# A bias table by distance: eight rows stored to DRAM, then spread to 128 rows by a DRAM-to-DRAM copy, issued in the first half of the projections

## The chip, the cores and the metric

The kernel runs on 1 core of one Trainium2 chip. The metric is the device time in microseconds (us) of one launch, as the median of 3 runs. One launch computes one inference step of a two-layer streaming encoder; weights, caches and inputs lie in DRAM at its start, and all outputs lie there at its end.

## The reference, cut to what matters

Layer 0 projects 2048 prompt frames and 64 sample frames, and mixes them in two branches. Branch A is latent attention (queries and keys are made by up-projections of small latents). Branch B is attention in a band of 9 chunks of 64 frames, with a learned bias per head that depends only on the clipped distance of query and key:

```
def _rel_bias(table, rel):                       # table: 8 heads x 257 distances
    idx = jnp.clip(rel, -B_MAX_REL, B_MAX_REL) + B_MAX_REL     # B_MAX_REL = 128
    return jnp.expand_dims(jnp.moveaxis(table[:, idx], 0, -3), -3)
...
    s = einsum(q, k) * scale + bias              # 64 queries x 576 keys, per head and chunk
```

Layer 1 is windowed attention without such a bias. What concerns the change is how the kernel gets the 8 x 257 table into a form from which it can load, for one head, a tile of 128 query rows whose row q is the row of biases shifted by q.

## The kernel before, in words

The program has five stages. Phase 1 projects the frames for layer 0; phase 2 is branch A, from about 845 us of the trace on; phase 3 is branch B with the output projection; two more do layer 1. All arithmetic on TensorE is done with each operand split in a high and a low part of float32r, and three products of them (`mm3`). All DMAs are issued by SyncE (`dma = nc.sync.dma_start`), one instruction after the other; an instruction that waits holds all behind it.

Phase 1 works in two halves of the frames, three chunks of 256 to 384 frames each. For a chunk, `norm_chunk` loads up to three tiles of 128 frames (tiles `R`, pool `raw`, 5 buffers, which the weight loads of `load_w` use too), takes sums of squares on ScalarE (line 251), makes the reciprocal roots on VectorE (`rstd_of`, lines 182 to 193), scales the rows (line 259), transposes them on TensorE (line 263) and splits them into the tile `X` (lines 207 and 210). Then come, for each half: the gate columns and the columns of the latent of the keys (`ckv`, 288 columns, tile `kcs` of rotary factors), the latent up-projections (`ukv`), the query latent (`qlat`) and its up-projection (`uq`), which loads a tile named `qcs` of rotary factors from a pool of one buffer, the queries and keys of branch B, its values (`vb`), and the last gate columns. Each result goes from PSUM (pool `pm`, 4 buffers) through a buffer of the pool `ev` (7 buffers) into a scratch tensor in DRAM: `sQA`, `sKA`, `sKR`, `sQR`, `sQB`, `sKB`, `sVB`, `sG`. A buffer of `ev` is free when its store has landed. The last keys of branch B are written out as a state too, by way of a transpose of an `ev` tile (line 489).

After the two halves, phase 1 makes the table `sE` (8 heads x 128 rows x 768 floats, 3 MB): the 257 biases of a head, reversed, go into partition h of a tile `e8` (named `qcs`, so it takes the same one buffer), VectorE repeats the first of them 511 times to the left (line 582), and one DMA writes each partition's row 128 times into `sE` (line 583). Phase 3 is its only reader; it loads `bias` tiles with a step that shifts row q by q.

The instructions are written in program order, but within phase 1 and across its border to phase 2 their order on each engine is set by the framework's planner, which simulates durations and issues what is ready first; phase 2's loads (lines 200, 622, 624, 637) are so put among phase 1's last stores. In phase 2 itself TensorE, VectorE and ScalarE follow the order as written.

Of the kernel before, what the change touches and what calls it, by code (L numbers as in the profile page):

```python
# [7 lines left out]
F32 = mybir.dt.float32  # L8
# [62 lines left out]
def tok_tiles(c0, n):  # L71
    r = []
    o = 0
    while o < n:
        w = min(128, n - o)
        r.append((c0 + o, o, w))
        o += w
    return r
# [29 lines left out]
def kernel(ctx, tc, a, o, upto=5):  # L108

    nc = tc.nc  # L110
    S = K()
    dma = nc.sync.dma_start
# [7 lines left out]
    def scratch(name, shape):  # L120
        return dr.tile(shape, F32, name=name)
# [9 lines left out]
    sQB = scratch("sQB", [2, 8, 64, SEQ])  # L131
    sKB = scratch("sKB", [2, 8, 64, SEQ])
    sVB = scratch("sVB", [8, SEQ, 128])
    sE = scratch("sE", [8, 128, 768])
    sM = scratch("sM", [512, T])
    sMB = scratch("sMB", [512, T])
# [31 lines left out]
    def load_row(t, src):  # L168

        dma(t, bass.AP(tensor=src.tensor, offset=src.offset, ap=[[0, 128], [1, t.shape[-1]]]))  # L170
        return t
# [40 lines left out]
    def load_w(pw, raw, src, kt, w, slot):  # L212

        W = pw.tile([128, slot], F32R, name="W")
        Wv = W[:, :2 * kt * w].rearrange("p (a k c) -> p a k c", a=2, k=kt)
        sv = src.rearrange("(k p) c -> p k c", p=128)
        step = max(1, 1024 // w)
        for k0 in range(0, kt, step):
            k1 = min(kt, k0 + step)
            R = raw.tile([128, 1024], F32, name="R")  # L220
            Rv = R[:, :(k1 - k0) * w].rearrange("p (k c) -> p k c", c=w)
            dma(Rv, sv[:, k0:k1])
            nc.scalar.activation(Wv[:, 0, k0:k1], Rv, AF.Copy)  # L223
            nc.gpsimd.tensor_tensor(Wv[:, 1, k0:k1], Rv, Wv[:, 0, k0:k1], op=ALU.subtract)  # L224
        return Wv

    def mm3(ps, lhs, rhs, kt):

        n = 3 * kt
        j = 0  # L230
        for k in range(kt):
            for x, y in TERMS:
                nc.tensor.matmul(ps, lhs(x, k), rhs(y, k), start=(j == 0), stop=(j == n - 1))  # L233
                j += 1
# [37 lines left out]
    def phase1():  # L272
        with ExitStack() as st:
            pool = pools(st, "right")
            lat, xin, rows, tb = pool("lat", 1), pool("xin", 2), pool("rows1", 1), pool("tb", 1)
# [8 lines left out]
            def first_loads():  # L284
                load_row(g_pre, a["ab_pre_norm"])
                dma(ident, a["ident"])

            def later_loads():
                load_row(g_kv, a["ab_kv_norm"])
                dma(kcs, a["krope"])  # L290
                load_row(g_q, a["ab_q_norm"])
# [13 lines left out]

            def ukv(W, cT, c_off, col0, n, vrow=None):


                for o0, w in even_split(n, 512, 64):
                    for j in range(4):  # L310
                        p = pm.tile([128, 512], F32, name="pm")
                        mm3(p[:, :w], lambda x, k: W[:, x, k, j * 128:(j + 1) * 128],
                            lambda y, k: cT[:, y, k, c_off + o0:c_off + o0 + w], 2)
                        hi = ev.tile([128, 512], F32R, name="ev")
                        lo = ev.tile([128, 512], F32R, name="ev")
                        copy(hi[:, :w], p[:, :w])
                        lo_of(lo[:, :w], p[:, :w], hi[:, :w])
                        for x, t in ((0, hi), (1, lo)):
                            dma(head_pair(sKA, x, j, col0 + o0, w), f(t[:, :w]))
                        yield  # L320

            def ukv_v(W, cT, c_off, t0, r, vrow):
                p = pm.tile([128, 512], F32, name="pm")
                mm3(p[:r], lambda x, k: cT[:, x, k, c_off:c_off + r], lambda y, k: W[:, y, k, 512:1024], 2)
                if vrow is None:
                    for h0 in (0, 4):
                        v_out(p[:, h0 * 64:h0 * 64 + 256], r, t0, None, h0, 4, sVA)
                else:
                    e = ev.tile([128, 512], F32, name="ev")
                    copy(e[:r], p[:r])  # L330
                    dma(sVS[vrow:vrow + r], e[:r])
# [170 lines left out]
            def build_x(c):  # L502
                Xs[c] = x_chunk(*c)

            def fs_piece(chunks, col, specs, after=None):
                for _ in fs_steps(chunks, col, specs, after):
                    pass

            def weave(main, other, lead, rate):

                acc = 0.0
                for i, _ in enumerate(main):
                    if i >= lead - 1:
                        acc += rate
                    while acc >= 1:
                        next(other, None)
                        acc -= 1
                for _ in other:
                    pass

            def latents(W, cT, hf):
                hb = HBASE[hf]
                yield from ukv(W, cT, 0, hb, HLEN[hf])
                for t0, off, r in tok_tiles(hb, HLEN[hf]):
                    ukv_v(W, cT, off, t0, r, 0 if t0 >= SEQ else None)
                    yield
                if hf == 1:
                    yield from cached(W)

            def fs_steps(chunks, col, specs, after=None):  # L530
                W = load_w(pw, raw, w_in[:, col:col + 128 * len(specs)], KT, 128 * len(specs), SLOT)
                for i, c in enumerate(chunks):
                    if c not in Xs:
                        build_x(c)
                    for jj, (kind, j) in enumerate(specs):
                        fs(W, Xs[c], jj, c[0], c[1], kind, j)
                        yield
                    if after:
                        build_x(after[i])

            build_x(CHUNKS[0])
            for hf in range(2):
                chunks, hb = HALVES[hf], HBASE[hf]
                main = fs_steps(chunks, 672, kinds[0:3])
                cT = lat.tile([128, 2, 2, 1088], F32R, name="lat")
                for i, c in enumerate(chunks):
                    for _ in range(3):
                        next(main)
                    if i == 0:
                        if hf == 0:  # L550
                            later_loads()
                        W = load_w(pw, raw, w_in[:, 384:672], KT, 288, SLOT)
                    if i + 1 < len(chunks) and chunks[i + 1] not in Xs:
                        build_x(chunks[i + 1])
                    ckv(W, Xs[c], c[0], c[1], cT, hb)
                main = fs_steps(chunks, 1056, kinds[3:6])
                next(main)
                W = load_w(pw, raw, a["w_ukv"], 2, 1024, SLOT)
                weave(main, latents(W, cT, hf), LD1[hf], RT1[hf])
                W = load_w(pw, raw, w_in[:, 0:384], KT, 384, SLOT)  # L560
                qT = lat.tile([128, 2, 3, 1088], F32R, name="lat")
                for c in chunks:
                    qlat(W, Xs[c], c[0], c[1], qT, hb)
                main = fs_steps(chunks, 1440, kinds[6:9])
                next(main)
                W = load_w(pw, raw, a["w_uq"], 3, 768, SLOT)
                weave(main, uq(W, qT, hb, chunks), LD2, RT2)
                fs_piece(chunks, 1824, kinds[9:12])
                for h0 in (0, 4):
                    W = load_w(pw, raw, w_in[:, 2208 + h0 * 64:2208 + h0 * 64 + 256], KT, 256, SLOT)  # L570
                    for c in chunks:
                        vb(W, Xs[c], c[0], c[1], h0)
                Ws = [load_w(pw, raw, w_in[:, col:col + 256], KT, 256, SLOT) for col in (2720, 2976)]
                for i, c in enumerate(chunks):
                    for j in range(4, 8):
                        fs(Ws[(j - 4) // 2], Xs[c], j % 2, c[0], c[1], "g", j)
                    if hf == 0:
                        build_x(HALVES[1][i])

            e8 = tb.tile([128, 768], F32, name="qcs")  # L580
            dma(e8[:8, 511:768], a["rel"])
            nc.vector.tensor_copy(e8[:8, 0:511], e8[:8, 511:512].to_broadcast([8, 511]))
            dma(sE, e8[:8, None].to_broadcast([8, 128, 768]))
            dma(o[11][448:512], vbs)
            for src, dst in ((a["cache_b_k"], o[10]), (a["cache_b_v"], o[11])):
                dma(dst[0:448], src[64:512])
# [1049 lines left out]
    def phase5():  # L1636

        with ExitStack() as st:
# [261 lines left out]
            with manual(M5, ORDERED | {mybir.EngineType.SP}):  # L1900
# [10 lines left out]
                J.tails.drain()  # L1911

    phase1()
    P3 = phase3()
    S.start3 = lambda: next(P3) if upto >= 3 else None
# [100 lines left out]
```

## Time and profile before

| | us |
|---|---|
| median of 3 runs | 2776.84 (2775.26 to 2778.05) |
| the profiled execution, its own time | 2781.05 |
| its span in the trace | 2779.1 |
| TensorE busy (matmul) | 2581.4, 93% of the span |
| VectorE, ScalarE, GpSimd busy | 1474.4, 1391.1, 774.1 |

[...] A busy share over 1 in the DMA column means that packets of several transfers overlap on an engine. GB/s counts what DRAM gave and what it took, so that a copy inside DRAM counts twice.

### The profile page before, as it was taken

The page shows a single profiled execution, that of the slowest core. Times are in us where ns is not written, and L with a number is a line of the kernel's source. Part 1 is how long each engine was busy: PE and PEld are TensorE (multiplying, and loading weights), DVE is VectorE, ACT ScalarE, POOL GpSimd, SP SyncE. Part 2 cuts the span into 40 slices and gives each one's busy share as a digit, 9 for nine tenths or more (in the row PEclk, how much of TensorE's full clock was granted, in tenths as well). Part 3 has the DMA queues.
Part 4 walks back from the last instruction along what each step waited for, and adds up shares of the span by engine and source line. Part 5 has one row for each costly group of instructions (what it writes and reads, how often), then busy time and mean ns, then how long its engine had stood idle before and what let it go on. Part 6 is the DMA issues. An engine that isn't in the chain of part 4 may idle for free. (4 is left out here: it accounts for less than half of the span.)

```text
span 2779.1 us, 46736 instructions
## 1 busy us (share of the span) xinstructions
PE 2581.4 (93%) x16296; PEld 2352.2 (85%) x16296; DVE 1474.4 (53%) x4048; ACT 1391.1 (50%) x3547; POOL 774.1 (28%) x1311
## 2 busy tenths in 40 slices
PE   7999999999399999999888989988999999999997
PEld 7999999898398888888757878878999998788886
DVE  5542155351006777777646777735213102788884
ACT  4332232422126777777656666652233222777784
POOL 1123222213012333321202313364213220244444
PEclk9999999999699999999979999999999998999999
DMA  6546444727626666662287776655535428455552
GB/s 200 169 146 206 127 140 142 240 87 201 137 89 172 181 190 176 189 179 77 70 252 191 191 195 184 194 188 188 170 101 169 130 68 244 103 132 136 144 132 70
DMA packets 382259, 437.91 MB, mean 158 GB/s; under 512 B 49920, under 2 KB 308872, under 8 KB 378792
## 3 DMA queue, kind: packets, MB, share of 16 engines
q1 hardware_dynamic: 382024, 434.92, 54.1%
q8 instruction: 130, 2.13, 0.3%
q14 instruction: 105, 0.86, 0.1%
HBM read 279.65 MB, written 157.07 MB: 157 GB/s over the span
## 5 line engine op out<-in xcount | busy, mean ns | idle before, releaser
L233 PE MATMUL pm<-X,W 128*128 128x384 f32 (+2 forms) x4536 | 752.8, 325 | 1.7 <-DVE ev L210 0.9
L233 PEld LDWEIGHTS pm<-X,W 128*128 128x128 f32 x4536 | 731.9, 189 | 4.4 <-DVE ev L210 1.1
L207 ACT ACTIVATE PT<-t 128x512 fp32r<-128x512 f32 (+3 forms) x704 | 343.8, 505 | 255.1 <-PE t L1192 96.2
L210 DVE SCALAR_TENSOR_TENSOR PT<-t,PT 128x512 fp32r<-128x512 f32 (+3 forms) x688 | 374.8, 569 | 97.9 <-ACT PT L207 95.2
L224 POOL TENSOR_TENSOR W<-R,W 128x768 fp32r<-128x768 f32 (+3 forms) x114 | 233.3, 2073 | 591.9 <-ACT W L223 539.2
L953 PE MATMUL proj<-Wo,MM 128*128 128x512 f32 (+1 forms) x1368 | 378.9, 406 | 4.2 <-POOL MM L1739 1.5
L210 DVE SCALAR_TENSOR_TENSOR ev<-pm,ev 128x384 fp32r<-128x384 f32 (+3 forms) x197 | 98.7, 503 | 518.6 <-ACT ev L1543 180.3
L233 PE MATMUL pm<-W,X 128*128 128x256 f32 (+5 forms) x2040 | 283.9, 299 | 0.7 <-DVE ev L210 0.7
L953 PEld LDWEIGHTS proj<-Wo,MM 128*128 128x128 f32 (+1 forms) x1368 | 235.4, 185 | 48.6 <-ACT z L207 4.6
L233 PEld LDWEIGHTS pm<-W,X 128*128 128x128 f32 (+1 forms) x2040 | 274.5, 188 | 2.1 <-DVE ev L210 0.9
L691 ACT ACTIVATE P<-s,m 128x512 f32<-128x512 f32 (+9 forms) x344 | 209.5, 616 | 32.6 <-DVE m L680 30.1
L672 PE MATMUL s<-KA,Q 128*128 128x512 f32 (+7 forms) x640 | 201.1, 397 | 9.1 <-ACT P L691 8.9
L715 PE MATMUL t<-ident,P 128*128 128x128 f32 x1088 | 176.3, 276 | 3.4 <-ACT P L691 1.0
L678 DVE TENSOR_REDUCE m<-s 128x1 f32<-128x480 f32 (+7 forms) x216 | 132.5, 613 | 81.0 <-PE s L672 80.6
L715 PEld LDWEIGHTS t<-ident,P 128*128 128x128 f32 x1088 | 134.7, 141 | 41.5 <-ACT P L691 15.0
L743 PE MATMUL acc<-PT,V 128*128 128x256 f32 x1152 | 156.1, 285 | 6.5 <-DVE OT L752 6.5
L743 PEld LDWEIGHTS acc<-PT,V 128*128 128x128 f32 x1152 | 140.4, 188 | 12.0 <-PE t L715 6.0
L207 ACT ACTIVATE ev<-pm 128x256 fp32r<-128x256 f32 (+7 forms) x117 | 51.3, 440 | 158.8 <-PE pm L233 72.1
L1686 ACT ACTIVATE P<-s,m 128x256 f32<-128x256 f32 (+2 forms) x264 | 119.7, 467 | 6.9 <-DVE m L1678 5.6
L223 ACT ACTIVATE W<-R 128x768 fp32r<-128x768 f32 (+3 forms) x114 | 97.9, 908 | 47.1 <-DMA R<-in_ab_w_in_dram 18.9
L1205 PE MATMUL acc<-PT,V 128*128 128x256 f32 x672 | 114.1, 302 | 4.9 <-DVE OT L1215 3.8
L672 PE MATMUL s<-KR,Q 128*128 128x384 f32 (+6 forms) x320 | 116.3, 363 | 2.1 <-DMA Q<-sQR 2.1
(249 smaller groups left out, 4068.3 us busy)
## 6 DMA issues: line engine op xcount, KB each, us to landing
Q<-sQA SPq DMA_DIRECT2D x128, 128.0 KB, 3.0
sWO<-W SPq DMA_DIRECT2D x32, 512.0 KB, 3.7
Q<-sQB SPq DMA_DIRECT2D x128, 128.0 KB, 3.4
Wo<-sWO SPq DMA_DIRECT2D x16, 1024.0 KB, 7.5
Q<-sQC SPq DMA_DIRECT2D x32, 512.0 KB, 7.7
R<-in_ab_w_in_dram SPq DMA_DIRECT2D x40, 384.0 KB, 3.8
K<-sKB SPq DMA_DIRECT2D x56, 256.0 KB, 5.4
V<-sVB SPq DMA_DIRECT2D x24, 512.0 KB, 6.4
```

What stands on the lines that cost most here:

```text
L207: nc.scalar.activation(out, in_, AF.Copy)
L210: nc.vector.scalar_tensor_tensor(out, x, scale, hi, op0=ALU.mult, op1=ALU.subtract)
L224: nc.gpsimd.tensor_tensor(Wv[:, 1, k0:k1], Rv, Wv[:, 0, k0:k1], op=ALU.subtract)
L233: nc.tensor.matmul(ps, lhs(x, k), rhs(y, k), start=(j == 0), stop=(j == n - 1))
L672: nc.tensor.matmul(s[:r, :n], self.Q[:, x, self.qo:self.qo + r], rhs, start=(x == 0), stop=(x == 2))
L678: nc.vector.tensor_reduce(m[:r, j:j + 1], s[:r, :n], axis=AX.X, op=ALU.max)
L691: nc.scalar.activation(self.P[:r, o0:o0 + n], self.s.pop(j)[:r, :n], AF.Exp, bias=self.m[:r, 6:7], accum_out=acc)
L715: nc.tensor.transpose(t[:, b], self.P[:, (b0 + b) * 128:(b0 + b + 1) * 128], ident)
L743: nc.tensor.matmul(acc[:, (i // 2) % 2], H.V[:, b0 + b], PT[:, x, b], start=(b0 + b == 0 and x == 0), stop=(b0 + b == i and x == 1))
L953: nc.tensor.matmul(p, M[:, x, k, :r], W[k][:, y, cs], start=(k == k0 and t == 0), stop=(k == k1 - 1 and t == 2))
L1205: nc.tensor.matmul(acc, self.H.V[:, self.base - self.H.b0 + b], self.PT[:, x, off + b], start=(b == 0 and x == 0), stop=(b == nblk - 1 and ...
L1686: nc.scalar.activation(self.P[:, c, :w], self.s[:, c, :w], AF.Exp, bias=m[:, 1, c:c + 1], accum_out=m[:, 0, c:c + 1])
```

## The change

A scratch tensor `sE1` of 8 x 768 floats is added. The table is made by a function `biases_by_distance`, called in the first half, after the weights of the latent up-projections are loaded: the tile `e8` is filled as before, its eight rows are stored once into `sE1` (24 KB), and `sE` is filled by one copy from DRAM to DRAM, whose outermost dimension is the 128 rows (source step 0), then the 8 heads, then 768 floats in a run. The five lines after the second half go.

```diff
+    sE1 = scratch("sE1", [8, 768])
     sE = scratch("sE", [8, 128, 768])
...
+            def biases_by_distance():
+
+                e8 = tb.tile([128, 768], F32, name="qcs")
+                dma(e8[:8, 511:768], a["rel"])
+                nc.vector.tensor_copy(e8[:8, 0:511], e8[:8, 511:512].to_broadcast([8, 511]))
+                dma(sE1, e8[:8])
+                dma(sE.rearrange("h q e -> q h e"),
+                    bass.AP(tensor=sE1.tensor, offset=sE1.offset, ap=[[0, 128], [768, 8], [1, 768]]))
...
                 W = load_w(pw, raw, a["w_ukv"], 2, 1024, SLOT)
+                if hf == 0:
+                    biases_by_distance()
                 weave(main, latents(W, cT, hf), LD1[hf], RT1[hf])
...
-            e8 = tb.tile([128, 768], F32, name="qcs")
-            dma(e8[:8, 511:768], a["rel"])
-            nc.vector.tensor_copy(e8[:8, 0:511], e8[:8, 511:512].to_broadcast([8, 511]))
-            dma(sE, e8[:8, None].to_broadcast([8, 128, 768]))
             dma(o[11][448:512], vbs)
```

Nothing else of the source differs, but the planner's order does. On SyncE, at the start of the program, before:

```order
L432 DMA qcs<-in_qrope_dram 128x2x384
L586 DMA out_dram<-in_cache_b_k_dram 16x14336
L586 DMA out_dram<-in_cache_b_v_dram 16x14336
L1524 DMA out_dram<-in_cache_c_k_dram 16x512
L1525 DMA out_dram<-in_cache_c_v_dram 16x512
L222 DMA R<-in_ab_w_in_dram 128x2x384 x2
L222 DMA R<-in_ab_w_in_dram 128x3x288 x2
L222 DMA R<-in_ab_w_in_dram 128x2x288
L249 DMA R<-in_x_prompt_dram 128x1024 x4
```

and in the changed kernel (`sE_67` is how the name `sE1` is printed there):

```order
L292 DMA qcs<-in_rel_dram 8x257
L593 DMA out_dram<-in_cache_b_k_dram 16x14336
L593 DMA out_dram<-in_cache_b_v_dram 16x14336
L1531 DMA out_dram<-in_cache_c_k_dram 16x512
L1532 DMA out_dram<-in_cache_c_v_dram 16x512
L223 DMA R<-in_ab_w_in_dram 128x2x384 x2
L294 DMA sE_67<-qcs 8x768
L223 DMA R<-in_ab_w_in_dram 128x3x288 x2
L223 DMA R<-in_ab_w_in_dram 128x2x288
L295 DMA sE<-sE_67 128x8x768
L442 DMA qcs<-in_qrope_dram 128x2x384
L250 DMA R<-in_x_prompt_dram 128x1024 x4
```

The planner has moved the three DMAs of the table ahead of the loads of the second chunk's frames (the four loads of `R` from the prompt: three tiles of chunk 2, one of chunk 3), well before the place at which the source names them.

On ScalarE, at the place where chunk 2's sums of squares (`sq`, with the number of the sums' tile, 344 before and 345 now) stand among the gate outputs (`ev`) and the latents' sums (`c`), before:

```order
L251 ACTIVATE sq,ss_344<-R 128x1024 x2
L475 ACT_TABLE_LOAD
L475 ACTIVATE ev<-pm 128x384
L251 ACTIVATE sq,ss_344<-R 128x1024
L475 ACTIVATE ev<-pm 128x384
L251 ACTIVATE sq,ss_691<-R 128x1024
L475 ACTIVATE ev<-pm 128x384
```

and now:

```order
L485 ACT_TABLE_LOAD
L485 ACTIVATE ev<-pm 128x384 x3
L252 ACTIVATE sq,ss_345<-R 128x1024
L363 ACTIVATE c,ss<-pm 128x256
L252 ACTIVATE sq,ss_345<-R 128x1024 x2
L363 ACTIVATE c,ss<-pm 128x256
L252 ACTIVATE sq,ss_692<-R 128x1024 x2
```

The sums of squares of chunk 2 now stand behind the three gate outputs and, for the last two, behind the first latent's sum. On VectorE the chain of chunk 2's roots (128x3), alone before, is now woven row by row with two chains of the latents (128x1).

On SyncE at the end of phase 1, among the stores of branch B's keys (`sKB`), before:

```order
L419 DMA sKB<-ev 128x384 x3
L583 DMA sE<-qcs 1024x1x768
L622 DMA KA<-sKA 64x2112
L419 DMA sKB<-ev 128x384
L624 DMA KR<-sKR 128x2112
L419 DMA sKB<-ev 128x384 x5
```

and now:

```order
L429 DMA sKB<-ev 128x384 x3
L644 DMA Q<-sQR 64x512 x2
L429 DMA sKB<-ev 128x384
L629 DMA KA<-sKA 64x1024
L429 DMA sKB<-ev 128x384
L629 DMA KA<-sKA 64x1024
L631 DMA KR<-sKR 128x1024
L629 DMA KA<-sKA 64x2112 x2
L429 DMA sKB<-ev 128x384
L631 DMA KR<-sKR 128x2112
```

The table's store is gone, and phase 2's loads of keys, part of which stood ahead of this place before, now stand here, closer together.

## Rows read from the trace of the kernel before

**Rows 1.** The page: span, and busy time of the engines.

```profile
span 2779.1 us, 46736 instructions
PE 2581.4 (93%) x16296; PEld 2352.2 (85%) x16296; DVE 1474.4 (53%) x4048; ACT 1391.1 (50%) x3547; POOL 774.1 (28%) x1311
```

**Rows 2.** Busy time by stretch around the end of phase 1; columns: stretch, its length, busy time and count on PE, PEld, DVE, ACT, POOL, then TensorE's granted clock, the DMA engines' share, GB/s.

```profile
673.00:677.00 4.00, 1.51 (x10) 1.19 (x9) 0.56 (x1) 1.17 (x3) 0.00 (x0) 1.00 0.79 231
...
690.00:741.00 51.00, 0.49 (x4) 0.23 (x2) 0.56 (x1) 0.12 (x1) 0.00 (x0) 0.56 0.53 92
741.00:747.00 6.00, 5.68 (x27) 5.68 (x28) 0.85 (x2) 3.82 (x10) 4.26 (x2) 0.51 0.66 212
```

**Rows 3.** Who waited for whom between 640 and 800 us, longest first; the last row is from the same view of SyncE's queue.

```profile
DVE ev L210 <- DMA sKB<-ev: 71.1, 3, 60.2
...
PE po L489 <- ACT ev L207: 53.3, 2, 50.8
SPq L419 <- DMA sE<-qcs: 12.9, 1, 12.9
```

**Rows 4.** SyncE's queue in order of time, 655 to 745 us: start, length of the issue, engine, line, operation, target<-source, count.

```profile
669.10 0.81 SPq L583 DMA_DIRECT2D sE<-qcs  x1
672.19 7.28 SPq L622 DMA_DIRECT2D KA<-sKA  x1
679.57 18.16 SPq L419 DMA_DIRECT2D sKB<-ev  x1
697.78 4.77 SPq L624 DMA_DIRECT2D KR<-sKR  x1
702.65 32.84 SPq L419 DMA_DIRECT2D sKB<-ev  x5
```

**Rows 5.** Time from issue to landing, in us, from the views of one tile: first the loads of phase 2's keys `KA` between 640 and 800 us (the longest is the one issued at 672.19), then the stores of branch B's keys `sKB` between 640 and 680 us.

```profile
DMA to landing us min/median/max: 7.3/7.7/65.3
...
DMA to landing us min/median/max: 2.9/8.1/9.2
```

**Rows 6.** TensorE in order of time, 670 to 760 us.

```profile
680.87 9.63 PE L233 MATMUL pm<-X,W 128*128 128x320 f32 x64
741.32 0.47 PE L489 MATMUL po<-ident,ev 128*128 128x128 f32 x1 [50.83 <-ACT ev L207]
741.45 8.02 PE L233 MATMUL pm<-W,X 128*128 128x256 f32 x45
...
755.86 3.11 PE L233 MATMUL pm<-W,X 128*128 128x256 f32 x24
```

**Rows 7.** Busy time by stretch, columns as in rows 2: three stretches at the program's start, then the burst of phase 2's loads, the table's store alone, the clock's fall and its rise.

```profile
4.00:6.00 2.00, 0.00 (x0) 0.00 (x0) 0.50 (x4) 1.15 (x2) 0.00 (x0) 1.00 0.90 212
13.00:14.00 1.00, 0.00 (x0) 0.00 (x0) 1.00 (x4) 0.05 (x1) 1.00 (x2) 1.00 1.91 787
...
30.00:32.00 2.00, 2.00 (x13) 2.00 (x13) 0.00 (x0) 0.68 (x2) 2.00 (x2) 1.00 0.82 244
...
667.00:670.00 3.00, 3.00 (x19) 3.00 (x18) 0.56 (x1) 0.49 (x1) 0.00 (x0) 1.00 1.16 368
...
691.00:694.00 3.00, 0.00 (x0) 0.00 (x0) 0.00 (x0) 0.00 (x0) 0.00 (x0) 1.00 0.46 49
694.00:697.00 3.00, 0.00 (x0) 0.00 (x0) 0.00 (x0) 0.00 (x0) 0.00 (x0) 0.78 0.46 49
...
745.00:748.00 3.00, 3.00 (x20) 3.00 (x20) 0.00 (x0) 0.48 (x2) 2.48 (x2) 0.69 0.59 171
```

**Rows 8.** The DMA view of 0 to 40 us: target<-source, count, KB each, median us from issue to landing. The first is a copy inside DRAM, the second a load of one row of 4 KB into 128 partitions.

```profile
out_dram<-in_cache_b_k_dram SPq DMA_DIRECT2D x1, 896.0 KB, 9.6
...
g_pre<-in_ab_pre_norm_dram SPq DMA_DIRECT2D x1, 512.0 KB, 5.4
```

**Rows 9.** The first 52 us in order of time: SyncE's queue, then ScalarE, VectorE and TensorE (four answers of the same view, columns as in rows 4).

```profile
13.02 10.23 SPq L222 DMA_DIRECT2D R<-in_ab_w_in_dram  x5
26.15 6.17 SPq L249 DMA_DIRECT2D R<-in_x_prompt_dram  x4
...
35.28 1.05 ACT L251 ACTIVATE sq<-R 128x1024 bf16<-128x1024 f32 x1
...
36.45 0.17 DVE L182 TENSOR_SCALAR rs<-ss 128x3 f32<-128x3 f32 x1 [12.25 <-ACT sq L251]
39.53 3.68 DVE L259 SCALAR_TENSOR_TENSOR R<-R,rs,g_pre 128x1024 f32<-128x1024 f32 x3
...
37.12 6.68 PE L233 MATMUL pm<-W,X 128*128 128x288 f32 x49
44.43 3.31 PE L233 MATMUL pm<-W,X 128*128 128x288 f32 x23
51.23 0.77 PE L233 MATMUL pm<-X,W 128*128 128x384 f32 x3
```

**Rows 10.** TensorE idle at the start, by stretch (columns as in rows 2), and the copy that fills the table's rows on VectorE, from the view of the tile `qcs`: duration in ns as min/median/max, first and last start, shapes.

```profile
11.20:18.40 7.20, 0.01 (x1) 0.04 (x1) 7.16 (x21) 1.85 (x4) 3.56 (x2) 1.00 1.03 394
...
L582 DVE COPY qcs<-qcs x1: 418/418/418, 662.9 to 662.9; 8x511 f32<-8x511 f32 x1
```

## The prediction

> **What bounds the kernel now.** I read the page first: TensorE is busy for 93% of the span [rows 1], so a change is worth what it takes from TensorE's idle time or adds to it. The table by stretch shows where that time lies: of the 51 us from 690 to 741, TensorE works 0.49 us, and just before, from 673 to 677, it misses 2.5 us [rows 2]. Next come the waits. The longest of that place is VectorE's, 60.2 us on the stores `sKB<-ev`; TensorE itself waits 50.8 us for an `ev` tile that ScalarE could not write; and SyncE's own queue names the table's store `sE<-qcs` as what it waited for [rows 3]. In order of time: the store is issued at 669.10, and the DMAs behind it hold SyncE for 7.28, 18.16, 4.77 and (five of them) 32.84 us [rows 4]. The load of `KA` issued at 672.19 lands 65.3 us later, at 737.5 [rows 5], and TensorE starts at 741.32 [rows 6]. So the reader is to see one chain: table store, then key stores behind it in the same queues, then no free `ev` buffer, then no PSUM to write. While the store runs alone the DMA engines are 0.46 busy and 49 GB/s arrive in DRAM [rows 7]. From its issue to 737.5 it takes some 67.6 us for 8 x 128 x 768 x 4 = 3.15 MB.
>
> **What the removal gives.** TensorE's idle time from 690 to 741, 51.00 - 0.49 = 50.5 us, and the 2.5 us before it [rows 2]. The clock was at its lower level when work came back (0.51 from 741 to 747): 45 matmuls of 256 columns took 8.02 us there and 24 of them 3.11 us at full speed later [rows 6], so 45 would take 5.8, and 2.2 us more come back. Together **55.2 us**. Nothing behind this point absorbs it: TensorE is near full again at once, and what follows only moves forward.
>
> **What is late next there.** With the store gone, phase 2's loads remain, and the order has them closer together: 256 + 512 + 2 x 528 KB between two key stores, then 1056 KB more. Already before, the burst brought the queues to a share of 1.16 and 368 GB/s [rows 7], and key stores took 8.1 us to land [rows 5]. The key pieces use three of the seven `ev` buffers for 24 matmuls, which last some 3.6 us (9.63 us for 64) [rows 6], so seven buffers cover 8.4 us. The 1.87 MB at 368 GB/s add 5.1 us to a landing, 8.1 + 5.1 - 8.4 = 4.8 us, and the 1.08 MB behind add something: I take **6 us**. It may be none, as TensorE lost just 2.5 us before; and it is at most the whole 2.95 MB at 212 GB/s, the slowest full stretch of loads [rows 7], 14 us. A gain below nothing is excluded here, since the 2.5 us are already counted as given back.
>
> **What the addition costs at the start.** The order puts the copy into `sE` on SyncE behind the fifth weight load, whose issue ended at 13.02 + 10.23 = 23.25 [rows 9]; say it starts at 24. Its sources are in place by then: the 24 KB store and the load of the table are small, and the fill of the rows costs VectorE 0.42 us [rows 10] in the chain that leads to the first matmuls, so **0.4 us**. Behind the copy, in the same queues, stand the rotary factors (384 KB) and the three tiles of chunk 2 (512 KB each).
>
> How long the copy runs is the open price, since no row shows a copy inside DRAM that reads the same rows again and again. Bounds from rows: at the best second of the copies of the caches, 787 GB/s read and written, so 393 copied [rows 7], 8.0 us; at the rate of one of them from issue to landing among other loads, 896 KB in 9.6 us [rows 8], 32.9 us. The nearest is the load of one DRAM row into 128 partitions, which filled most of 4 to 6 us at 212 GB/s (5.4 us to land) [rows 7, 8]: 14.8 us. I take that, since it too reads the same bytes 128 times over in runs of a few KB.
>
> Then 1.97 MB at 244 GB/s, the rate at which these tiles came before [rows 7], are 8.1 us: the third tile lands at 24 + 14.8 + 8.1 = 46.9, and its sum of squares (1.05 and the read of the sum) is ready at 48.1, against 36.45 [rows 9]. From there to the first gate matmul of chunk 2 it took 51.23 - 36.45 = 14.8 us before: 3.1 for the root's chain, 3.7 for the scaling, 8.0 for transposes and splits. Now the chain is woven with two others, 46 short operations in place of 15 (5 us, between 3.1 if the others hide and 6.9 at 0.15 each), and the transposes, no longer held by TensorE's order, begin 2.5 us earlier beside the scaling: 5 + 3.7 + 8.0 - 2.5 = 14.2. So 62.3 against 51.2: **11.1 us**, of which TensorE's work that needs no chunk 2, done at 44.43 + 3.31 = 47.7 [rows 9], hides no more than it did. Even with an instant copy the order of ScalarE costs: the sums of tiles 2 and 3 stand behind the first latent's sum, that is behind 24 of the matmuls that begin at 37.12, some 40.4, then 0.4 and two sums, 43.2; plus 14.2 is 57.4, **6.2 us**. A copy under some 10 us is hidden up to there.
>
> TensorE stands idle for 6 to 7 us at this place. Before, the clock fell some 5 us into the long idle stretch (0.78 in 694 to 697) [rows 7], and the return cost 2.2; but 7.2 us without work at the program's start left it at 1.00 [rows 10]. I take half, **1.1 us**, with 0 and 2.2 as ends.
>
> [...]
>
> **The sum.** -55.2 + 6 + 11.1 + 0.4 + 1.1 = -36.6 us. On the profiled execution that is 2781.05 - 36.6 = 2744; the median lies 4.2 below that execution, so I forecast **2740 us**. All at the good ends: -55.2 + 0 + 6.2 + 0.4 = -48.6, 2728. All at the bad ends: the third tile at 24 + 32.9 + 8.1, start cost 29.2, burst 14, clock 2.2: -9.4, 2767.
>
> **The rivals.** *First, only the number of engines counts.* The old store ran on about eight engines at 49 / 8 = 6 GB/s each; if that pace per engine is what a copy of many short runs gets, sixteen take 67.6 / 2 = 33.8 us. Then the third tile lands at 65.9 and the start costs 30.1: -55.2 + 6 + 30.1 + 0.4 + 2.2 = -16.5, **2760**. [...] Against it: ordinary loads in rows of 4 KB reach 368 GB/s, 23 for each engine [rows 7], so the pace of 6 came from somewhere else.
>
> *Second, on the other side: all engines read the same 24 KB of DRAM and get in each other's way.* If the copy is no faster than the old store, 67.6 us, the frames of chunk 2 come that much later, the start costs 63.9, and the sum is +17.3, **2794**. It turns slower than before once the copy takes more than some 50 us. For it speaks only that nothing here was read from so few bytes in such a volume; against it the 212 GB/s of the one-row load [rows 7].
>
> *Third, phase 2's burst of loads was half the stall.* If key stores keep waiting behind `KA`, `KR` and `Q`, some 30 us stay: -55.2 + 30 + 12.6 = -12.6, **2764**. For it: the share of 1.16 ahead of the table's store. Against: TensorE was busy through that burst, and during the stall the rate was the store's 49 GB/s.
>
> *Fourth, the start costs little.* The copy runs at the best rate and just the order's 6.2 us remain, burst 3: -55.2 + 3 + 6.2 + 0.4 = -45.6, **2731**. For it: the caches' copies at 787; against: their runs are far longer than 3 KB.
>
> That the change does not do what it says is seen in part already: the planner issues the copy at some 24 us, not at the up-projections, which come after all three chunks of the half. The sums above have it there.
>
> **How the numbers follow.** Forecast (2733 to 2750) 0.62; start nearly free 0.16; engine count alone 0.12; burst 0.05; crowding in DRAM 0.05. Reaching out until two in ten are left gives 2727 to 2760. A measurement here tells 0.2%, 5.6 us, from no change. Faster by more than that: 0.62 + 0.16 + 0.12 + 0.05 less a remnant, 0.94; slower takes most of the crowding, 0.04; the same 0.02.
>
> **What would show it.** In the profile after: no stretch of TensorE under half busy near 690; key stores that land within some 13 us; first gate matmul of chunk 2 near 62 (57 for the fourth rival, 81 for the first); SyncE's waits without `sE`. I am wrong if TensorE stalls again at 670 to 700, or if chunk 2's tiles land later than 60.

## The result and the profile after

The changed kernel takes **2737.01 us** (median; 2729.1 to 2739.07) against 2776.05 of the kernel before in the same comparison: ratio **0.9854** [0.9833, 0.9875]. The forecast was 2740 in a range of 2727 to 2760. The profiled execution took 2738.16 us, against the 2781.05 from which the prediction counted, that is 42.9 less; the sum had said 36.6 less. By the medians it is 39.0 less: the execution of the kernel before that was profiled lies 5.0 us above its median. One execution of 8767.61 us, in experiment 7 below, is left out of its median and its ratio. The page of the profile after, span and busy time, answers to [rows 1]:

```profile
span 2735.9 us, 46737 instructions
PE 2586.1 (95%) x16296; PEld 2354.4 (86%) x16296; DVE 1470.0 (54%) x4048; ACT 1392.3 (51%) x3547; POOL 777.3 (28%) x1311
```

TensorE's own work is no shorter than before (2586.1 against 2581.4 us); all that came back is idle time. (All line numbers of the program are some 1 to 10 higher after the edit: L210 is L211, L419 is L429, L489 is L499.)

**Where it came back.** Busy time by stretch at the end of phase 1 in the kernel after, columns as in [rows 2]:

```profile
685.00:688.00 3.00, 2.49 (x17) 2.22 (x16) 0.00 (x0) 0.00 (x0) 0.00 (x0) 1.00 0.96 187
688.00:691.00 3.00, 0.00 (x0) 0.00 (x0) 0.00 (x0) 0.00 (x0) 0.00 (x0) 0.86 0.99 243
691.00:694.00 3.00, 0.96 (x4) 0.96 (x5) 0.00 (x0) 0.66 (x2) 0.00 (x0) 0.50 1.01 353
694.00:697.00 3.00, 3.00 (x13) 3.00 (x12) 0.16 (x1) 0.00 (x0) 0.00 (x0) 0.50 0.72 191
697.00:700.00 3.00, 3.00 (x23) 3.00 (x22) 0.27 (x1) 1.41 (x5) 0.00 (x0) 1.00 0.67 208
```

The hole of 51 us is one of 5.6. While TensorE stands still, the DMA engines are now full (0.99 and 1.01, 243 and 353 GB/s), where they had been 0.46 busy at 49 GB/s [rows 7]: what is left is a wait behind loads that run at speed. The first two waits of [rows 3] are there again from 640 to 800 us in the kernel after (total, times, longest), their longest at a fifth and a ninth of what it was, and SyncE no longer waits for the table. ScalarE's row, the second here, had a longest of 59.2 us in the kernel before:

```profile
DVE ev L211 <- DMA sKB<-ev: 19.1, 3, 12.9
...
ACT ev L208 <- DMA sKB<-ev: 10.7, 3, 8.7
```

```profile
PE po L499 <- ACT ev L208: 5.6, 1, 5.6
```

The second fence is the same view for TensorE alone. In the view of the tile `sKB` after, 640 to 800 us, a key store lands after a median of 3.5 us, the slowest after 14.9:

```profile
DMA to landing us min/median/max: 2.3/3.5/14.9
```

**What it cost at the start.** The kernel after, 12 to 32 us: SyncE's queue, then ScalarE, then TensorE in order of time (columns as in [rows 9]):

```profile
17.34 6.02 SPq L223 DMA_DIRECT2D R<-in_ab_w_in_dram  x3
23.45 0.59 SPq L295 DMA_DIRECT2D sE<-sE  x1
24.10 0.67 SPq L442 DMA_DIRECT2D qcs<-in_qrope_dram  x1
25.43 6.14 SPq L250 DMA_DIRECT2D R<-in_x_prompt_dram  x4
```

```profile
40.39 1.06 ACT L252 ACTIVATE sq<-R 128x1024 bf16<-128x1024 f32 x1 [3.48 <-DMA R<-in_x_prompt_dram]
...
41.45 0.37 ACT L363 ACTIVATE c<-pm 128x256 f32<-128x256 f32 x1
...
42.98 1.06 ACT L252 ACTIVATE sq<-R 128x1024 bf16<-128x1024 f32 x1
43.94 0.18 ACT L252 ACTIVATION_READ_ACCUMULATOR sq<-R 128x1 f32 x1
```

```profile
36.23 9.75 PE L234 MATMUL pm<-W,X 128*128 128x288 f32 x72
49.69 0.47 PE L385 MATMUL po<-ident,k 128*128 128x128 f32 x1 [3.71 <-POOL k L377]
...
58.06 1.09 PE L234 MATMUL pm<-X,W 128*128 128x384 f32 x3
```

The copy is issued at 23.45. In the trace's records of packets its 1024 pieces of 3 KB run from 25.1 to 35.4 us, 10.3 us. ScalarE waits for chunk 2's first tile until 40.39, and from there it works through: a square, the latent's sum at 41.45, two more squares, as the order said. The third sum is read at 44.1, and 14.0 us later, at 58.06, comes chunk 2's first gate matmul; before it was 51.23 [rows 9]. Matmul for matmul, the kernel after is 6.8 us late from there on, some 6 late by 480 us, 42.0 early behind the old hole, and 43.2 early at the end. (The matmuls of the two traces are compared by their place in the order of starts.)

### The profile page after: what moved, and what is told of

It is laid out like the page before. It is cut to its first block, busy times and chain, and to the rows that moved or that the text cites. A ratio compares the mean times of both kernels' runs of the same rounds, so it can differ in the third digit from the quotient of the medians.

```text
span 2735.9 us, 46737 instructions
## 1 busy us (share of the span) xinstructions
PE 2586.1 (95%) x16296; PEld 2354.4 (86%) x16296; DVE 1470.0 (54%) x4048; ACT 1392.3 (51%) x3547; POOL 777.3 (28%) x1311
## 4 chain that ended last, share of the span: by engine, by line
PE 74%; DVE 10%; DMA 6%; ACT 4%; issue 3%; POOL 2%; SPq 1%; ACTq 0%; DVEq 0%; POOLq 0%
PE pm L234 37%; PE proj L960 9%; PE s L679 6%; PE acc L750 4%; PE t L722 3%; DVE PT L211 2%; PE acc L1212 2%; PE s L1172 2%; PE t L1702 2%; PE t L1199 2%; PE acc L1709 2%; PE s L1681 1%; ACT P L698 1%; DVE m L685 1%; DVE s L1684 1%
## 5 line engine op out<-in xcount | busy, mean ns | idle before, releaser
L211 DVE SCALAR_TENSOR_TENSOR PT<-t,PT 128x512 fp32r<-128x512 f32 (+3 forms) x688 | 374.5, 568 | 100.1 <-ACT PT L208 97.4
L211 DVE SCALAR_TENSOR_TENSOR ev<-pm,ev 128x384 fp32r<-128x384 f32 (+3 forms) x197 | 98.7, 502 | 474.5 <-ACT ev L1550 180.3
L960 PEld LDWEIGHTS proj<-Wo,MM 128*128 128x128 f32 (+1 forms) x1368 | 236.1, 186 | 49.2 <-ACT z L208 4.6
L722 PEld LDWEIGHTS t<-ident,P 128*128 128x128 f32 x1088 | 134.6, 141 | 41.4 <-ACT P L698 14.9
L1684 DVE CUSTOM_DVE_ANT_0 s<-s,mask 128x256 f32<-128x256 f32 (+1 forms) x256 | 107.4, 422 | 16.3 <-PE s L1681 5.8
```

Source lines behind the costliest of these rows:

```text
L211: nc.vector.scalar_tensor_tensor(out, x, scale, hi, op0=ALU.mult, op1=ALU.subtract)
L722: nc.tensor.transpose(t[:, b], self.P[:, (b0 + b) * 128:(b0 + b + 1) * 128], ident)
L960: nc.tensor.matmul(p, M[:, x, k, :r], W[k][:, y, cs], start=(k == k0 and t == 0), stop=(k == k1 - 1 and t == 2))
L1684: nc.vector.tensor_tensor_reduce(s[:, c, :w], s[:, c, :w], mk, 1.0, -3e38, ALU.add, ALU.max, m[:, 0, c:c + 1])
```

## The experiments

Each ratio is to the kernel before, run on the same chip in the same comparison.

**1. The new way at the old place.** Both DMAs as in the kernel after, called behind the second half, where the old store stood.

```diff
-                if hf == 0:
-                    biases_by_distance()
...
+            biases_by_distance()
             dma(o[11][448:512], vbs)
```

> The new path alone, at the old place: the eight rows go to DRAM and the copy with 128 rows outermost fills the table, but behind the second half, where the store stood. Pace theory (what counts is how long the transfer holds the queues; the copy takes some 10 us, as in the changed kernel, the old store 61): no delay at the start, TensorE idles some 8 to 15 us near 690 in place of 50, time 2736 (2730 to 2746). Place theory (a transfer of 3 MB in the middle of phase 2's loads stalls the key stores by whatever path it comes): 30 us or more of the stall stay, 2755 or more.

Measured: 2727.96 us, 0.9826 [0.9811, 0.984], less than the 2730 to 2746 that were expected, since TensorE waits some 5 us there and not 8 to 15. The hole is a wait of 3.2 us at 671 and one of 1.8 at 697, by stretch:

```profile
668.00:672.00 4.00, 3.48 (x21) 3.16 (x19) 0.00 (x0) 0.00 (x0) 0.00 (x0) 1.00 0.98 267
672.00:676.00 4.00, 1.36 (x7) 1.36 (x8) 1.11 (x2) 1.26 (x3) 0.00 (x0) 0.91 1.04 276
...
696.00:700.00 4.00, 2.21 (x15) 2.00 (x15) 0.42 (x1) 1.10 (x4) 0.07 (x1) 0.89 0.74 225
```

The first of these waits is over (674.64) before the copy is issued (674.89), so not even all of this is the copy's. The old place was never the trouble; the pace was. The move to the start gave next to nothing here and cost 6.8 us there. A measure that leaves out the rest of the program, used below too, is the time from the matmul that starts at 640 us in the kernel before to the one that starts at 760, by their place in the order: 120.0 us in the kernel before, 71.9 in the kernel after, 72.8 here.

**2. The same copy on half of the engines.** As 1, but with the 8 heads outermost.

```diff
-                dma(sE.rearrange("h q e -> q h e"),
-                    bass.AP(tensor=sE1.tensor, offset=sE1.offset, ap=[[0, 128], [768, 8], [1, 768]]))
+                dma(sE, bass.AP(tensor=sE1.tensor, offset=sE1.offset, ap=[[768, 8], [0, 128], [1, 768]]))
```

> As the kernel before in place, but the table is copied from the eight rows in DRAM with the 8 heads outermost, so on eight engines. Theory of engine count alone: eight engines go at the old store's pace, 458 ns for a packet of 3 KB, 58 us, and the time is that of before, 2776. [...]

Measured: 2734.1 us, 0.9849 [0.9834, 0.9864], 6.1 us above experiment 1, and 41.9 below the 2776 of engine count alone. The DMA view of 680 to 684 us, where nearly all packets are the copy's (packets and their mean rate; queue, packets, MB, share of the 16 engines):

```profile
DMA packets 277, 0.84 MB, mean 210 GB/s; under 512 B 1, under 2 KB 6, under 8 KB 277
...
q1 hardware_dynamic: 277, 0.84, 52.0%
```

The share is 8.3 of 16 engines, where the copy with 128 rows outermost came to a share of 1.027 (26 to 28 us of the kernel after), so the order of dimensions does confine it. But 4 us x 16 x 0.520 / 277 is 120 ns for a packet, and 210 GB/s is more than four times the old store's 49 [rows 7] on as many engines. TensorE's second wait grows from 1.8 to 5.0 us:

```profile
697.20 4.58 PE L234 MATMUL pm<-W,X 128*128 128x256 f32 x21 [4.95 <-ACT ev L208]
```

From 640 to 760 as above it takes 75.8 us, 3.0 more than experiment 1. The rest of the 6.1 is not seen at this place. Behind 760, where the source is the same, the two profiled executions took 2011.6 and 2005.0 us, with 109 and 89 us of it at the lower clock. So the number of engines is worth some 3 us here, and a few us of a difference in the total can lie elsewhere, where the clock differs from execution to execution.

**3. The old store, its rows spread over partitions.** The kernel before, still from SBUF with the eight rows outermost, which lie in partitions 0, 4, ..., 28 in place of 0 to 7.

```diff
-            dma(e8[:8, 511:768], a["rel"])
-            nc.vector.tensor_copy(e8[:8, 0:511], e8[:8, 511:512].to_broadcast([8, 511]))
-            dma(sE, e8[:8, None].to_broadcast([8, 128, 768]))
+            nc.gpsimd.memset(e8[:32, 511:768], 0.0)
+            dma(e8[0:32:4, 511:768], a["rel"])
+            nc.vector.tensor_copy(e8[:32, 0:511], e8[:32, 511:512].to_broadcast([32, 511]))
+            dma(sE, e8[0:32:4, None].to_broadcast([8, 128, 768]))
```

> The kernel before, its store out of SBUF at the old place and on eight engines, but the eight rows lie in partitions 0, 4, 8 to 28 in place of 0 to 7 (GpSimd zeroes the columns of the unused partitions, VectorE fills 32 partitions in place of 8). Theory of engine count alone: unchanged, 458 ns a packet, 61 us, 2776. Theory of neighbouring partitions: packets of 121 to 230 ns, 16 to 30 us, most of the stall goes, 2740 to 2756.

Measured: 2727.85 us, 0.9824 [0.9809, 0.9838], level with experiment 1 with no copy from DRAM, and below the 2740 to 2756 that its theory had expected. Its 1024 packets take a median of 121 ns in the trace's records and are through at 688. In the kernel before it was 458 ns, and the DMA view of 691 to 694 us, with the store alone, agrees (3 us x 16 x 0.459 / 48 = 459 ns):

```profile
q1 hardware_dynamic: 48, 0.15, 45.9%
```

By stretch, where TensorE's two longest waits are (3.7 us at 670, 3.4 at 688; 1.9 more follow):

```profile
668.00:672.00 4.00, 2.15 (x13) 1.83 (x11) 0.00 (x0) 0.00 (x0) 0.00 (x0) 1.00 0.97 295
672.00:676.00 4.00, 2.19 (x8) 2.19 (x9) 1.12 (x2) 2.08 (x6) 0.00 (x0) 0.65 0.87 306
...
688.00:692.00 4.00, 0.58 (x4) 0.58 (x4) 0.56 (x1) 0.38 (x1) 0.00 (x0) 0.78 0.63 240
```

From 640 to 760 as above it takes 78.2 us, 5.4 more than experiment 1; in the profiled execution the part behind 760 is shorter again (1997.8 us, with 82 at the lower clock). So of the 47.2 us that experiment 1 gained at this place, the rows' new partitions by themselves gave 41.8. What made the old store slow was that its rows lay in partitions 0 to 7: 458 ns a packet there, 121 from 0, 4, ..., 28. Why rows in the first came more slowly, no run shows.

**4. The old store at the new place.**

```diff
-                dma(sE1, e8[:8])
-                dma(sE.rearrange("h q e -> q h e"),
-                    bass.AP(tensor=sE1.tensor, offset=sE1.offset, ap=[[0, 128], [768, 8], [1, 768]]))
+                dma(sE, e8[:8, None].to_broadcast([8, 128, 768]))
```

> The new place alone: the old store out of SBUF, eight engines, made in the first half. Pace theory: the store holds the queues for 61 us ahead of chunk 2's tiles, so the third lands at about 90 and the first gate matmul of chunk 2 comes at 100 to 108 in place of 58; the stall near 690 is gone but for the 6 us of the changed kernel: 2737 + 42 to 50 = 2779 to 2787, level with the kernel before or slower. Place theory: anywhere but among phase 2's loads will do, 2737 to 2745.

Measured: 2786.27 us, 1.0037 [1.0026, 1.0049], slower than before by 10 us, as expected (2779 to 2787). The stall has moved: by stretch at the start, then the longest wait of ScalarE from 10 to 110 us, SyncE's queue in order of time, and the DMA view of 55 to 58 us:

```profile
40.00:50.00 10.00, 0.00 (x0) 0.00 (x0) 0.00 (x0) 0.00 (x0) 0.00 (x0) 0.53 0.63 93
50.00:60.00 10.00, 0.00 (x0) 0.00 (x0) 0.00 (x0) 0.00 (x0) 0.00 (x0) 0.50 0.47 49
```

```profile
ACT W L223 <- DMA R<-in_ab_w_in_dram: 49.7, 2, 49.4
```

```profile
17.13 0.83 SPq L293 DMA_DIRECT2D sE<-qcs  x1
18.02 50.10 SPq L222 DMA_DIRECT2D R<-in_ab_w_in_dram  x3
```

```profile
q1 hardware_dynamic: 48, 0.15, 46.5%
```

The same 49 GB/s as in [rows 7], 3 us x 16 x 0.465 / 48 = 465 ns a packet, and a weight load behind it in the queues arrives 50 us late. Chunk 2's work is 59 us late (its first gate matmul at 110.00, where 100 to 108 was expected, against 51.23 [rows 9]), and the hole at 690 is gone but for 4.5 us. This is the prediction's second rival, by a store that truly is that slow: it priced the start at 63.9 us.

**5. The table in the second half.** The kernel after with one digit changed.

```diff
-                if hf == 0:
+                if hf == 1:
                     biases_by_distance()
```

> The changed kernel with the table made in the second half instead of the first; the planner then issues the copy among the last key stores of the first half, and the order at the program's start is that of the kernel before. Theory (the 6.8 us at the start come from the copy standing ahead of chunk 2's tiles and from the order planned around it): first gate matmul of chunk 2 back at 51, the copy of 10 us mostly under the cover of the seven buffers, the rest as in the changed kernel: 2737 - 6.8 + 0 to 4 = 2730 to 2734. Rival (the copy costs as much wherever it stands, since stores wait behind it): 2736 to 2740.

Measured: 2725.88 us, 0.982 [0.9803, 0.9837], below the 2730 to 2734 that were expected. The planner again issues the copy ahead of its place, at 262.02 us, among key stores of the first half. By stretch around it, then at the end of phase 1:

```profile
260.00:264.00 4.00, 4.00 (x25) 4.00 (x24) 0.56 (x1) 0.49 (x1) 0.00 (x0) 1.00 1.08 312
264.00:268.00 4.00, 4.00 (x25) 4.00 (x24) 0.56 (x1) 0.49 (x1) 0.00 (x0) 1.00 0.88 296
268.00:272.00 4.00, 4.00 (x25) 4.00 (x24) 0.56 (x1) 0.49 (x1) 0.00 (x0) 1.00 1.01 319
272.00:276.00 4.00, 4.00 (x30) 4.00 (x30) 0.00 (x0) 0.49 (x1) 0.00 (x0) 1.00 1.03 309
...
680.00:684.00 4.00, 1.53 (x11) 1.27 (x9) 0.00 (x0) 0.00 (x0) 0.00 (x0) 1.00 1.00 307
684.00:688.00 4.00, 2.58 (x10) 2.59 (x11) 0.00 (x0) 0.66 (x2) 0.00 (x0) 0.61 0.95 307
```

TensorE does not miss a microsecond while the copy runs, although the DMA engines are full. The start is as before (chunk 2's first gate matmul at 50.81), and behind the old hole the matmuls come 49.4 us early, 7.3 more than in the kernel after: some 6 that were left of the start's 6.8, and 1.4 by a wait of 3.9 us in place of 5.6 (70.5 us from 640 to 760). The medians are 11 us apart; what is over lies behind 760, where these runs don't say why. This version has the lowest median, level with experiments 1 and 3 by their intervals, and clear of the next one, which ran on the same chip and has the early copy.

**6 and 7. More buffers for the stores.** The pool `ev` with 8 buffers in place of 7 (two in place of three of the small `e2`, whose name the views print as `e`), in the kernel after and in experiment 5.

```diff
-            px, pw, raw, ev = pool("px", 3), pool("pw", 2), pool("raw", 5), pool("ev", 7)
+            px, pw, raw, ev = pool("px", 3), pool("pw", 2), pool("raw", 5), pool("ev", 8)
...
-                        e2 = ev.tile([128, 128], F32, name="e2", bufs=3)
+                        e2 = ev.tile([128, 128], F32, name="e2", bufs=2)
```

> The changed kernel with eight buffers of the pool ev in place of seven (the tile e2 has two buffers in place of three, to make room). Theory (what is left of the stall near 690 is key stores that land 13 us late against a cover of 8.4 us by seven buffers): one buffer more covers 1.2 us more, so 5.5 us of idle time become some 4 and the clock perhaps does not fall: 2733 to 2736. Rival (SyncE held by the loads of Q sets it): no change, 2737.

> Both: the table made in the second half and eight buffers of ev. By the theories of the two, 2726 to 2733; if they do not add, the time of the one with the table in the second half alone.

Measured: 2737.11 us, 0.9867 [0.9852, 0.9881], and 2726.42 us, 0.9824 [0.9808, 0.9839]: no gain from either. The first came where its rival had it (2737, no change), but not by the rival's cause: TensorE's wait has another name in both, and lasts 4.1 us in the first (5.6 in the kernel after) and 8.8 in the second (3.9 in experiment 5); its rows in order of time, one from each, are

```profile
697.66 0.51 PE L499 MATMUL po<-ident,ev 128*128 128x128 f32 x2 [4.11 <-ACT e L208]
...
691.25 0.69 PE L499 MATMUL po<-ident,ev 128*128 128x128 f32 x2 [8.79 <-ACT e L208]
```

The `ev` tiles no longer hold it; the small tiles `e` do, of which the edit had taken one away. So these two runs don't tell whether the number of `ev` buffers limits the end of phase 1, only that this trade is worth nothing.

## Why the prediction came out right, point by point

**The pace was the cause** (the first theory): shown. At the old place a fast way gives 0.9826 or 0.9824 (1, 3), at the new place the slow way gives 1.0037 (4). Of the two things that the old store had against it, eight engines and neighbouring partitions, the partitions carry nearly all, 41.8 of 47.2 us at this place (3), and the engines 3.0 to 5.4 (2, 3). The count of eight engines agrees with the shares (0.46 of 16, 7.4, for the old store [rows 7], and 8.3 in 2), but would by itself have missed the cause: it expected 2776 of both runs, which took 2734.1 and 2727.85.

**The end of phase 1**: -55.2 + 6 = -49.2 predicted, -48.1 measured (from 6.0 late to 42.0 early). By parts: the waits of 2.5 and 50.8 us became one of 5.6, which gives 47.7; the clock's 2.2 us did not come back, since the short wait also took the clock down (0.50 from 691 to 697, with work from 693). The residual of 6 was right for the idle time, and the clock's price belonged to it. The prediction's own mark "no stretch under half busy near 690" failed, and contradicted that term: 6 us of waiting have to stand somewhere. The same goes for its sign of being wrong, a stall at 670 to 700 us: taken by the letter there is one, from 687.5 to 693.0, of the size that the sum had put at 6. The other mark, landings within some 13 us, holds but for one store (14.9).

**The start**: 11.1 + 0.4 + 1.1 = 12.6 predicted, 6.8 measured. This is the mis-sized term, and the size that was off is the copy's: 14.8 us taken from a load into SBUF, 10.3 measured. The third sum came at 44.1 in place of 48.1, and so the first gate matmul 4.2 us earlier than forecast; the rest of the 5.8 between are the 0.4 us for the fill of the table's rows, not seen by itself, and the clock's 1.1. The way from the third sum to the first gate matmul was foreseen at 14.2 us and took 14.0. That matmul came at 58.06, close to the 57.4 of the order's floor and the fourth rival, but by another way: the floor is lower in the kernel after. The latents' matmuls begin at 36.23 and the 24th is done at some 39.5 (9.75 us for 72), so with the tiles in place the latent's sum and two squares would have had the third sum read at some 42.2, an estimate from these rows; the tiles, with the copy in front of them, made it 44.1. So the order by itself would have cost some 5 of the 6.8 us, and the tiles by themselves, three squares from 40.39 on, nearly all of it, both estimates with the 14.0 as it is. No run took away one and kept the other.

**The clock's 1.1 us**: not found as a term of its own. The granted clock did fall after TensorE's wait at 46, as these stretches of the kernel after show, but VectorE worked through most of that time, and TensorE, at 0.50, was idle for 2.2 of 8 us. Eight transposes took 1.97 us there and 1.04 at full speed in experiment 5; whether that lengthened the chain, which took 14.0 us in all, is not shown:

```profile
46.00:48.00 2.00, 0.00 (x0) 0.00 (x0) 2.00 (x23) 1.08 (x2) 0.00 (x0) 1.00 0.01 5
48.00:50.00 2.00, 0.31 (x2) 0.31 (x3) 2.00 (x6) 0.00 (x0) 1.35 (x1) 0.62 0.24 74
50.00:58.00 8.00, 5.79 (x26) 4.67 (x24) 6.05 (x15) 3.43 (x7) 0.27 (x1) 0.50 0.42 99
```

**The rivals.** Engine count alone (2760): falls, by 2. Crowding in DRAM (2794): falls; 1024 packets that read the same 24 KB take a median of 121 ns, as fast as those of experiment 3 that read SBUF. The burst as half of the stall (2764): falls, since 5.6 us of waiting are left beside the same loads. The start nearly free (2731): near in its size at the start (6.2 against 6.8), though the tiles and not the order alone set it, and its burst of 3 us too small; the result lies between it and the forecast.

**What was luck.** Against the medians the sum is off by 2.4 us (36.6 and 39.0), although the start was priced 5.8 too high and the end 1.1 too favourably. The rest of the gap lies outside both places, where the executions differ by some us, so the sum is less exact than its total looks.

**Open**: what sets the size of the 4 to 6 us that remain. The trace's records of landings show what they wait for. In the kernel after, ScalarE's 8.7 us end when the key store issued at 680.30 lands, at 692.52, and the load of `KA` issued just ahead of it (679.61) landed at 692.35; TensorE returns at 693.04. In experiment 5 the same two land at 684.90 and 684.72, and TensorE returns at 685.42. So the key stores wait behind phase 2's loads of keys, as the prediction's residual had it; the four loads of `Q`, which hold SyncE for 7.34 us from 682.50, were issued behind that store. Why the wait is 5.6 in one and 3.9 in the other is not shown; no run moved these loads.

## What to carry to other kernels

Before a slow transfer is moved out of the way, ask why it is slow: here one that used half of the engines at 49 GB/s was slow by the partitions from which its rows came, and spreading eight rows over partitions 0, 4, ..., 28 gave 41.8 of the 47.2 us that the copy on all engines gave at the old place. If it is moved all the same, look in the planner's order for what stands behind it in the queue: at 23 us it cost 6.8, at 262 us nothing. And where a wait for loads is the last one left, a sum that names its idle time should price the clock with it: here a wait of 5.6 us, to 693.0, came with a granted clock of 0.50 from 691 to 697.

## What the runs showed of the hardware

A packet of 3 KB took 458 ns (464 in experiment 4) when some eight engines (a share of 0.46) read rows from partitions 0 to 7, and 121 ns from partitions 0, 4, ..., 28, or from 24 KB of DRAM that are read 128 times over (medians). With all engines that copy came to 393 GB/s in its best stretch, one packet in 2 us x 16 x 1.027 / 256 = 128 ns (DMA view of the kernel after, 26 to 28 us):

```profile
DMA packets 256, 0.79 MB, mean 393 GB/s; under 512 B 0, under 2 KB 0, under 8 KB 256
...
q1 hardware_dynamic: 256, 0.79, 102.7%
```

These rows also correct the text ahead of the prediction, which said that a copy inside DRAM counts twice in GB/s: 256 packets of 3 KB are 0.79 MB, so it counts once. Nor is the best stretch of the caches' copies, 787 GB/s at a share of 1.91 [rows 7], a rate of copying. These views count a packet where it starts: nine of the caches' 32 packets, of 57,344 bytes each, start from 13 to 14 us and make 0.52 of the 0.79 MB there, but each lasts 2.1 us or more. Spread over the time that they took, the packets of that stretch come to 410 GB/s at a share of 1.05, so a share far over 1 need not mean that packets overlap as much, though some do: from 667 to 670 us of the kernel before, 17 to 21 packets are under way at once in the trace's records, for 16 engines, during 1.7 of the 3 us. At 57,344 bytes in 2.116 us, the shortest, an engine would copy 27 GB/s and sixteen 434, and 3.15 MB would take 7.3 us, estimates from this packet alone; the prediction's lower bound for the copy, 8.0, came near this by two errors that cancel. Since in its sums the order hides a copy of under some 10 us, none of its numbers rested on it, but the fourth rival's argument from the 787 falls.
